# Seven block products instead of eight for gate and up of the first FFN, with weight sums on GpSimd and activations normalised ahead

## The chip, the cores and the metric

The kernel runs on one core of one Trainium2 chip. The profile names five engines: PE (TensorE, matmuls, with the weight loads as PEld), DVE (VectorE), ACT (ScalarE), POOL (GpSimd) and SP (SyncE, which here only issues DMAs). Matrix products land in PSUM banks, everything else lies in SBUF; weights and activations come from HBM by DMA. The metric is device time in microseconds of one execution, the median of several.

## The reference, cut to what matters

One layer of a hybrid decoder for 512 prompt tokens and 8 x 4 sample tokens, 544 in all, in float32:

```python
def swiglu(x, wg, wu, wd):
    return (jax.nn.silu(x @ wg) * (x @ wu)) @ wd

def layer(h, ...):
    h = h + 0.5 * rmsnorm(swiglu(rmsnorm(h, norm_g[0]), wg[0], wu[0], wd[0]), norm_g[1])
    m, c_kv, k_r, s_fin = mixer(rmsnorm(h, norm_g[2]), ...)
    h = h + rmsnorm(m, norm_g[3])
    h = h + 0.5 * rmsnorm(swiglu(rmsnorm(h, norm_g[4]), wg[1], wu[1], wd[1]), norm_g[5])
    return h, c_kv, k_r, s_fin
```

`wg` and `wu` are 1024 x 2816, `wd` is 2816 x 1024. The mixer (a gated linear recurrence beside latent attention over a paged cache) is the same in both kernels.

## The kernel before

Activations are kept transposed: 128 features on the partitions, tokens along the free axis, so `h[x]` is 128 x 8 x tokens. The 544 tokens are two halves, `x` = 0 of 256 and `x` = 1 of 288 (names ending in `a` and `b`). Float32 accuracy comes from splitting each operand in a high part, rounded to the matmul's type, and the remainder: `uh`/`ul` for activations, `wh`/`wl` for weights. A product of two split operands is three matmuls (high x high, high x low, low x high), written by `mm3`, `gemm` and `gemm_q` (L253, L271). One weight block of 1024 x 128 is loaded to `wraw` (five buffers, DMA on SP's queue), cast to `wh` on ACT (L244) and subtracted to `wl` on DVE (L245) by `weight`. So a block times one half of the tokens is 8 x 3 = 24 matmuls into one PSUM bank `acc`.

Start (scope `xin`): tokens are loaded as rows (`xt`), transposed by PE (L420) and copied to `h` (L423). Of the first norm only the gain is applied before the products (`split_u`, L202 and L203); the factor per token (`rstd_u`, L176 to L193) is worked out beside the first products and applied to their results (L343, and by the square in `post`).

The first FFN (`ffn`) runs in chunks of 8, 7 and 7 blocks of 128 hidden features. For each block: gate for both halves, up for both halves, then silu and product (`sil`, `sit`, L343 to L346, sigmoid as exp, ln, exp on ACT at L313 to L315) and a split into `hh`/`hl` (L165, L166). After a chunk, eight down groups, one per 128 output features, add into `mT` (`ma`, `mb`; L369 the first time, L371 later). In the last chunk the last five output features are taken half by half (staged weights `whx`, `wlx`), so that `post` can normalise the first half, add it to `h` (L305, L306) and make the mixer's `u` while PE works on the second half. Then the mixer starts with three weight blocks on half 0 and on half 1 (`zx`, L586).

The order of instructions on each engine is fixed at build time: a scheduler lays the program's operations out on in-order queues, and each waits there for its operands and for its buffers. SP's queue holds all weight loads in the order of use.

Of the kernel before, what the change touches and what calls it, by code (L numbers as in the profile page):

```python
# [8 lines left out]
F32 = mybir.dt.float32  # L9
# [17 lines left out]
HM = max(HS)  # L27
DFF = 2816
NF = DFF // P
FCH = (((0, 8), (8, 7), (15, 7)), ((0, 6), (6, 6), (12, 5), (17, 5)))  # L30
# [75 lines left out]
def hybrid_step_kernel(  # L106
# [14 lines left out]
    halves = (slice(0, HS[0]), slice(HS[0], T))  # L121
    BOTH = (0, 1)
# [22 lines left out]
    def actslot(name, x, dt=F32, shape=None):  # L145
        return mk(shape or [P, KD, HS[x]], dt, name + "ab"[x], pool=act)
# [3 lines left out]
    h = [actslot("h", x) for x in BOTH]  # L150

    def hslices(lo, n):
        out = []
        for x in BOTH:
            o = halves[x].start
            a, b = max(lo, o), min(lo + n, halves[x].stop)
            if a < b:
                out.append((x, slice(a - o, b - o), slice(a - lo, b - lo)))
        return out
# [45 lines left out]
    def parted_u(norm, x):  # L205
        u = actslot("uh", x, F32R), actslot("ul", x, F32R), tmp("rn" + "ab"[x], HS[x], 1)
# [91 lines left out]
    def post(x, mT, acc, r, nxt=None):  # L298
        s = tmp("s_post", HS[x])
# [3 lines left out]
        for k in range(0, KD, 2):  # L303
            ks = slice(k, k + 2)
            nc.vector.tensor_tensor(mT[:, ks], mT[:, ks], s[:, None, :].broadcast_to([P, 2, HS[x]]), op=ALU.mult)  # L305
# [3 lines left out]
            if k == 2:  # L309
                yield  # L310
# [93 lines left out]
    newb = mk([P, TS], BF16, "newb")  # L404
    with scope("xin"):
# [4 lines left out]
        nc.vector.tensor_copy(gv, pv[:, :V_N])  # L410

        def xload(tiles):
            for i in tiles:
# [3 lines left out]
                for q in range(2):  # L417
# [3 lines left out]
                    for x, dst, src in hslices(i * P, n):  # L421
                        eng = nc.scalar.copy if q else nc.vector.tensor_copy
                        eng(h[x][:, 4 * q : 4 * q + 4, dst], px.rearrange("p (k t) -> p k t", k=4)[:, :, src])  # L423

        w0, u0 = [], {}

        def first(c):
            w0.append(weight([wcols((w_g, w_u)[c][0], 0, KD, 0)], KD))

        xload((0, 1))  # L430
        if W0 == 0:
            first(0)
        u0[0] = split_u(0, 0)
        if W0 == 1:
            first(0)
        xload((2, 3, 4))
        first(1)
        u0[1] = split_u(0, 1)
        nc.vector.tensor_scalar_mul(gq, gv[:, 0:48], 0.5)
        for x in BOTH:  # L440
            rstd_u(u0[x], x)
# [26 lines left out]

    stg = ExitStack()
    st = stg.enter_context(tc.tile_pool(name="st", bufs=1, side="right", reuse_waits="tile"))  # L470
    with scope("ffn0"):
        U = [None, None]
        hsp = [dr.tile([P, KD, HS[x]], F32, name="hsp%d" % x, tag="hsp%d" % x) for x in BOTH]

        def to_mix(x):
            U[x], part = parted_u(2, x)
            return part

        first_w = []

        def mid():
            first_w.extend(weight([wcols(w_in, 0, KD, 2048 + i * P)], KD, True) for i in JOBS[:NST])

        for _ in ffn(0, 1, BOTH, u0, to_mix, mid):
            pass
        for x in BOTH:
            nc.sync.dma_start(hsp[x], h[x])
# [5 lines left out]
    def fetch(x, slot, src):  # L493
        h[x] = mk([P, KD, HS[x]], F32, slot, pool=act)
# [8 lines left out]
    def project(x, nxt=None):  # L503
        fetch(x, ("q0", "hb")[x], hsp[x])
# [30 lines left out]
    with scope("mix") as mx_:  # L535
# [5 lines left out]
        q0 = mk([P, 2, KQ, HS[0]], F32R, "q0", pool=act)  # L541
        q1 = mk([P, 2, KQ, HS[1]], F32R, "q1", pool=dK)
        qh, ql = (q0[:, 0], q1[:, 0]), (q0[:, 1], q1[:, 1])
        s_q = [mk([P, HS[x]], F32, "s_q%d" % x) for x in BOTH]

        def cq(j, a, x):
            scaled_split(qh[x][:, j], ql[x][:, j], a, gcol(V_QG + j))
            q = tmp("sq1", HS[x])
# [4 lines left out]
        def kvz(j, a, x):  # L553
            nc.scalar.copy(zkv[:, j, halves[x]], a)
# [27 lines left out]
        zx = [ps("zx")[:, : HS[1]] for _ in first]  # L582
# [19 lines left out]
        def hgrn(hd):  # L602
            def zcol(z, off):
                w = weight([wcols(w_in, 0, KD, off + hd * P)], KD)
                for x, hs in enumerate(halves):
# [216 lines left out]
        with scope("at2"):  # L822
# [7 lines left out]
            with scope("kv"):  # L830
# [5 lines left out]
                for x, hs in enumerate(halves):  # L836
# [603 lines left out]
```

## Time and profile before

| | |
|---|---|
| median of three runs | 1312.4 us (1311.62, 1312.40, 1316.96) |
| profiled execution: span, first to last instruction | 1312.7 us |
| its own time around the span | not listed apart; the span lies 0.3 us above the median |
| PE busy | 1288.4 us, 98% |
| DVE busy | 879.7 us, 67% |
| ACT busy | 713.9 us, 54% |
| POOL busy | 73.8 us, 6% |
| mean granted TensorE clock | 0.995 |
| HBM traffic over the span | 145 GB/s |

In a row of groups there stand the line, the engine, the operation, the output and the inputs, the shape (partitions x elements), the count, then busy time and mean duration of one, then the idle time in front and what ended it. Matmuls overlap one another, so the mean duration of a matmul is longer than the distance from one start to the next. A timeline row begins with the start and the duration in us. A row of a table by stage gives the stretch, its length, then busy time and number of instructions of PE, PEld, DVE, ACT and POOL, then the granted clock, the DMA engines' share and GB/s; a table cut to one line of code leaves out engines that have nothing there.

### The profile page before, as it was taken

How to read it: one execution, taken by the hardware profiler on the slowest of the kernel's cores; microseconds unless marked ns; L12 is line 12 of the kernel's file. 1: busy time of each engine (PE TensorE's matmuls, PEld its weight loads, DVE VectorE, ACT ScalarE, POOL GpSimd, SP SyncE). 2: the span in 40 equal slices, each digit the busy share in tenths (PEclk: the TensorE clock that was granted, in tenths of full speed). 3: DMA queues.
4: the chain of work that ended last, by engine and by line, in shares of the span. 5: the costliest groups of instructions: out<-in, count | busy, mean ns of one | idle time of the engine just before them, and what ended most of it. 6: DMA issues, size and time to landing. Idle time of an engine off the chain costs nothing.

```text
span 1312.7 us, 30501 instructions
## 1 busy us (share of the span) xinstructions
PE 1288.4 (98%) x12696; PEld 1196.2 (91%) x12696; DVE 879.7 (67%) x1765; ACT 713.9 (54%) x1503; POOL 73.8 (6%) x80
## 2 busy tenths in 40 slices
PE   7999999999999999999999999999999999999998
PEld 6999999999999988888987888878788999999997
DVE  7553244435457787875867789899987878466664
ACT  6543344324455644544758656665656677554454
POOL 0000000000000000000000222232310000000000
PEclk9999999999999999999999999999999999999998
DMA  7323233332353223333223687988886746656451
GB/s 217 90 81 96 82 88 85 85 98 81 88 154 113 95 65 84 84 85 114 59 86 96 239 285 244 300 276 278 283 268 183 222 137 178 177 144 186 137 158 55
DMA packets 280552, 192.87 MB, mean 147 GB/s; under 512 B 12765, under 2 KB 271422, under 8 KB 275550
## 3 DMA queue, kind: packets, MB, share of 16 engines
q1 hardware_dynamic: 271920, 147.65, 39.0%
q0 software_dynamic: 7168, 41.95, 8.7%
q8 instruction: 100, 1.64, 0.5%
q10 hardware_dynamic: 1326, 1.32, 0.3%
q14 instruction: 38, 0.31, 0.1%
HBM read 181.22 MB, written 9.67 MB: 145 GB/s over the span
## 4 chain that ended last, share of the span: by engine, by line
PE 85%; DVE 6%; ACT 5%; DMA 3%; issue 1%; SPq 0%; DVEq 0%; ACTq 0%
PE acc L253 54%; PE acc L271 16%; PE s L1141 3%; PE o L1174 2%; DVE wl L245 1%; ACT wh L244 1%; PE s L954 1%; PE pa L693 1%; DMA wraw<-w_d 1%; PE acc L282 1%; DMA wraw<-w_u 1%; PE zx L586 1%; ACT pbuf L1165 1%; PE pr L186 1%; PE o L986 1%
## 5 line engine op out<-in xcount | busy, mean ns | idle before, releaser
L244 ACT CAST wh<-wraw 128x1024 fp32r<-128x1024 f32 (+3 forms) x255 | 248.2, 976 | 296.4 <-PE acc L253 238.3
L245 DVE TENSOR_TENSOR wl<-wraw,wh 128x1024 fp32r<-128x1024 f32 (+3 forms) x255 | 288.7, 1133 | 147.9 <-ACT wh L244 147.4
L253 PE MATMUL acc<-uhb,wh 128*128 128x288 f32 x768 | 227.6, 296 | 0.6 <-ACT uhb L202 0.6
L253 PE MATMUL acc<-ulb,wh 128*128 128x288 f32 x768 | 227.1, 296 | 0.0
L253 PE MATMUL acc<-uhb,wl 128*128 128x288 f32 x768 | 225.7, 294 | 0.8 <-DVE wl L245 0.7
L271 PE MATMUL acc<-uha,wh 128*128 128x256 f32 x528 | 158.3, 301 | 1.0 <-ACT uha L202 1.0
L271 PE MATMUL acc<-uha,wl 128*128 128x256 f32 x528 | 149.7, 284 | 2.3 <-DVE wl L245 2.3
L271 PE MATMUL acc<-ula,wh 128*128 128x256 f32 x528 | 150.3, 285 | 0.0
L253 PEld LDWEIGHTS acc<-uhb,wl 128*128 128x128 f32 x768 | 144.4, 188 | 1.3 <-DVE wl L245 1.3
L253 PEld LDWEIGHTS acc<-uhb,wh 128*128 128x128 f32 x768 | 144.1, 188 | 1.4 <-ACT uhb L202 0.8
L253 PEld LDWEIGHTS acc<-ulb,wh 128*128 128x128 f32 x768 | 144.2, 188 | 0.1
L253 PE MATMUL acc<-uha,wh 128*128 128x256 f32 x416 | 117.8, 283 | 0.5 <-DVE sil L343 0.5
L253 PE MATMUL acc<-uha,wl 128*128 128x256 f32 x416 | 117.5, 283 | 0.7 <-DVE wl L245 0.7
L253 PE MATMUL acc<-ula,wh 128*128 128x256 f32 x416 | 117.2, 282 | 0.2 <-DVE ula L203 0.2
L271 PEld LDWEIGHTS acc<-uha,wh 128*128 128x128 f32 x528 | 99.8, 189 | 16.3 <-issue 14.0
L271 PEld LDWEIGHTS acc<-uha,wl 128*128 128x128 f32 x528 | 100.4, 190 | 3.7 <-DVE wl L245 3.2
L271 PEld LDWEIGHTS acc<-ula,wh 128*128 128x128 f32 x528 | 100.5, 191 | 1.1 <-issue 1.0
L253 PE MATMUL acc<-hhb,wh 128*128 128x288 f32 x317 | 93.5, 297 | 0.6 <-ACT hhb L165 0.6
L253 PE MATMUL acc<-hlb,wh 128*128 128x288 f32 x317 | 93.9, 297 | 0.1
L253 PE MATMUL acc<-hhb,wl 128*128 128x288 f32 x317 | 92.9, 294 | 0.0
L253 PEld LDWEIGHTS acc<-uha,wl 128*128 128x128 f32 x416 | 78.3, 188 | 1.1 <-DVE wl L245 1.1
L253 PEld LDWEIGHTS acc<-uha,wh 128*128 128x128 f32 x416 | 78.4, 188 | 0.8 <-DVE sil L343 0.8
(483 smaller groups left out, 2926.4 us busy)
## 6 DMA issues: line engine op xcount, KB each, us to landing
wraw<-w_g SPq DMA_DIRECT2D x66, 512.0 KB, 4.5
wraw<-w_u SPq DMA_DIRECT2D x66, 512.0 KB, 4.0
wraw<-w_in SPq DMA_DIRECT2D x24, 512.0 KB, 4.0
wraw<-w_d SPq DMA_DIRECT2D x32, 384.0 KB, 4.4
wraw<-w_d SPq DMA_DIRECT2D x32, 320.0 KB, 3.3
wraw<-w_o SPq DMA_DIRECT2D x16, 512.0 KB, 4.1
wraw<-w_d SPq DMA_DIRECT2D x16, 448.0 KB, 3.8
wraw<-w_d SPq DMA_DIRECT2D x8, 512.0 KB, 4.0
```

What stands on the lines that cost most here:

```text
L186: nc.tensor.matmul(pr[:, :n], ones, acc, start=True, stop=True)
L244: nc.scalar.copy(wh[:, :kt], w[:, :kt])
L245: nc.vector.tensor_tensor(wl[:, :kt], w[:, :kt], f32(wh[:, :kt]), op=ALU.subtract)
L253: nc.tensor.matmul(out, a, b, start=n == 0, stop=n == last)
L271: nc.tensor.matmul(acc[:, :n], a[:, k], b[:, k], start=k + i == 0, stop=k == kt - 1 and i == 2)
L282: nc.tensor.matmul(acc, a[:, k], b[:, k], start=k + i == 0, stop=k == kt - 1 and i == 2)
L586: nc.tensor.matmul(z, w[a][:, k], U[1][b][:, k], start=k + n == 0, stop=k == KD - 1 and n == 2)
L693: nc.tensor.matmul(pa[es, c * 32 : (c + 1) * 32].rearrange("p (n m) -> p n m", m=m), kx[:, cs], up(qx[:, cs]), start=True, stop=True, skip ...
L954: nc.tensor.matmul(s[:, :N], qa[a_], ka[b_], start=n == 0, stop=False, skip_group_check=True)
L986: nc.tensor.matmul(o[:, lo : 2 * P], a_[:, k, hs], b_[:, k, lo:], start=n == 0, stop=n == 3 * q0 + 5, skip_group_check=True)
L1141: nc.tensor.matmul(self.s[r][c * 32 : c * 32 + 32, :P], q[rs, j], kh, start=st + jj == 0, stop=st == len(JS) - 1 and jj == 1, skip_group_c ...
L1174: nc.tensor.matmul(o[g : g + 32, :R], self.p[:, c, a], self.craw[c][:, a], start=i + c == 0 and a < 4, stop=i + c == 2 and a >= 4, skip_gr ...
```

## The change

Gate and up of the first FFN are worked out in pairs of blocks. For a pair, the weights are a 2 x 2 matrix of blocks (lower and upper four of the eight k tiles by first and second column block, `w1` and `w2`), and the activations another (lower and upper k tiles by first and second half of the tokens). Seven products of sums replace the eight block products (Winograd's form of Strassen's scheme). The halves become even, 272 and 272, all through the first FFN and the mixer's first stages; `project` and the second FFN keep 256 and 288.

- `xin`: each token row is squared and summed on ACT (L452), its factor made by Ln and Exp, spread over the partitions by a matmul with the identity (L456) and copied to `rb` (L457); `ux` = `h` times gain times factor (L462, L467), then split. `h` is written out to HBM (`hx`) and its slots (`ha`, `hb`) hold the gate and up results, until it is loaded again for `post`.
- `classic`: the first pair of gate and of up still takes 96 matmuls. Beside it the four activation sums are built (L598, two on POOL, two on DVE) and split to T1 to T4.
- `seven`: four sums of weight blocks on POOL (L541 to L544), seven splits of 128 x 512 (cast on ACT L168, subtraction on DVE L169), seven products of 12 matmuls (L536) into the banks X, Y and Z, two copies out of X (L562, L566) and five additions (L559). `issue_after` ties the later splits behind the previous pair's first copy.
- `gated`: sigmoid, two products and the split, for both halves at once (128 x 544; L318 to L320, L584, L585).
- Chunks of 6, 6, 6 and 4 blocks instead of 8, 7 and 7.

On DVE inside gate/up, there stood for each block two splits of 1024, and for each half three steps of the gating and a split:

```order
L343 TENSOR_TENSOR sil<-acc,rna 128x256
L345 TENSOR_TENSOR sil<-sil,sit 128x256
L343 TENSOR_TENSOR sil<-acc,rnb 128x288
L245 TENSOR_TENSOR wl<-wraw,wh 128x1024
L345 TENSOR_TENSOR sil<-sil,sit 128x288
L346 TENSOR_TENSOR sil<-sil,acc 128x256
L166 TENSOR_TENSOR hla<-sil,hha 128x256
L346 TENSOR_TENSOR sil<-sil,acc 128x288
```

Now, for the gate of one pair at a chunk's start (`ha` is the gate's result, `Y` and `Z` banks, `tq` the copy of X, `S` the sums from POOL, `s4` the last of them):

```order
L559 TENSOR_TENSOR ha<-Y,tq 128x272
L169 TENSOR_TENSOR wl<-S,wh 128x512 x2
L559 TENSOR_TENSOR ha<-Y,tq 128x272
L559 TENSOR_TENSOR ha<-Z,ha 128x272
L169 TENSOR_TENSOR sl<-wraw,sh 128x512 x2
L559 TENSOR_TENSOR ha<-Y,tq 128x272
L169 TENSOR_TENSOR sl<-wraw,sh 128x512 x2
L559 TENSOR_TENSOR ha<-Z,ha 128x272
```

The additions that empty the banks now stand between splits, some of which take POOL's results.

On ACT at the start, before (up to the first half's `u`):

```order
L448 ACTIVATE lbe<-lbe 128x8
L423 COPY ha<-px 128x4x128
L244 CAST wh<-wraw 128x1024
L423 COPY ha<-px 128x4x128
L202 ACTIVATE uha<-ha,gv 128x256 x8
```

and now, from the second token tile on (`xq` is a scratch output, `rows` the sums and factors):

```order
L452 ACTIVATE xq,rows<-xt 128x1024
L449 COPY ha<-px 128x4x128
L454 ACTIVATE rows<-rows 128x1
L453 ACTIVATE rows<-rows,epst 128x1
L479 ACTIVATE lbe<-lbe 128x8
L168 CAST wh<-wraw 128x1024
L449 COPY ha<-px 128x4x16
L449 COPY hb<-px 128x4x112
L454 ACTIVATE rows<-rows 128x1
L168 CAST sh<-wraw 128x1024
L452 ACTIVATE xq,rows<-xt 128x1024
L168 CAST uha<-ma 128x272 x5
```

The casts of the first half now stand behind the Squares and behind two weight casts.

On POOL, whose queue held nothing between the mask cast and the mixer, each `seven` now has four operations in a row (`S` the sums, `wraw` overwritten in place):

```order
L541 TENSOR_TENSOR S<-wraw 128x512
L542 TENSOR_TENSOR S<-S,wraw 128x512
L543 TENSOR_TENSOR wraw<-wraw 128x512
L544 TENSOR_TENSOR S<-wraw,S 128x512
```

Each waits for the one ahead or for both weight blocks; the splits above wait for them.

The core of the diff:

```diff
+W2 = T // 2
+WARM = 1
-FCH = (((0, 8), (8, 7), (15, 7)), ((0, 6), (6, 6), (12, 5), (17, 5)))
+FCH = (((0, 6), (6, 6), (12, 6), (18, 4)), ((0, 6), (6, 6), (12, 5), (17, 5)))
...
+                sq = mk([P, D], F32, "xq", 2)
+                r = rows[:n, i : i + 1]
+                nc.scalar.activation(sq[:n], xt[:n], AF.Square, accum_out=r)
+                nc.scalar.activation(r, r, AF.Ln, scale=1.0 / D, bias=epst[:n])
+                nc.scalar.activation(r, r, AF.Exp, scale=-0.5)
+                pr = ps("pr")
+                nc.tensor.matmul(pr[:, :n], r.broadcast_to([n, P]), ident[:n, :n], start=True, stop=True)
+                nc.vector.tensor_copy(rb[:, i * P : i * P + n], pr[:, :n])
...
+        for k in range(KD):
+            nc.vector.scalar_tensor_tensor(ux[0][:, k], h[0][:, k], gcol(k), rb[:, even[0]], op0=ALU.mult, op1=ALU.mult)
+            split(UB[0][0][:, k], UB[0][1][:, k], ux[0][:, k])
...
-        for _ in ffn(0, 1, BOTH, u0, to_mix, mid):
-            pass
...
+        def product(bank, a, b, first):
+            for k in range(4):
+                for n, (p, q) in enumerate(((0, 0), (0, 1), (1, 0))):
+                    nc.tensor.matmul(bank, a[p][:, k], b[q][:, k], start=first and k + n == 0, stop=k == 3 and n == 2, skip_group_check=True)
...
+        def seven(w, C, mid=None):
+            w1, w2 = w
+            S = mk([P, 3, 4, P], F32, "S", 2)
+            nc.gpsimd.tensor_tensor(S[:, 0], w2[:, lo4], w2[:, hi4], op=ALU.add)
+            nc.gpsimd.tensor_tensor(S[:, 1], S[:, 0], w1[:, lo4], op=ALU.subtract)
+            nc.gpsimd.tensor_tensor(w2[:, lo4], w1[:, lo4], w2[:, lo4], op=ALU.subtract)
+            nc.gpsimd.tensor_tensor(S[:, 2], w1[:, hi4], S[:, 1], op=ALU.subtract)
+            a, s, v = ring(), ring(), ring()
+            for ks in (lo4, hi4):
+                split(*parts(a, ks), w1[:, ks])
+            for i, ks in enumerate((lo4, hi4)):
+                split(*parts(s, ks), S[:, i])
+            s4 = [mk([P, 4, P], F32R, "s4" + n, 2, pool=sp) for n in "hl"]
+            with tc.issue_after(mark[0]):
+                for ks in (lo4, hi4):
+                    split(*parts(v, ks), w2[:, ks])
+                split(*s4, S[:, 2])
...
+            product(X, parts(a, lo4), B11, True)
+            mark[0] = nc.scalar.copy(t, X).ins
+            product(Y, parts(s, hi4), T2, True)
+            plus(1, Y, t)
+            product(X, parts(a, hi4), B21, False)
+            nc.scalar.copy(C[:, 0], X)
...
+            product(Y, parts(v, lo4), T3, False)
+            plus(3, Y, t)
+            product(Z, parts(s, lo4), T1, True)
+            plus(3, Z, C[:, 3])
+            product(Y, parts(v, hi4), T4, False)
+            plus(2, Y, t)
+            product(Z, s4, B22, False)
+            plus(1, Z, C[:, 1])
...
+                    seven(raw_pair(w_g[0], f0 + j), G, (lambda: split(*T4, r[0])) if f0 + j == 2 * WARM else None)
+                    if late:
+                        with tc.issue_after(mark[0]):
+                            gated(*late)
+                    seven(raw_pair(w_u[0], f0 + j), V)
+                late = j, G, V
+            gated(*late)
```

200 lines of the change are left out of this document (147 added, 53 removed).

## The prediction

> **What bounds the kernel now.** I read the page's busy times and chain first, then a table by stage, then the timeline inside one stage.
>
> ```profile
> span 1312.7 us, 30501 instructions
> PE 1288.4 (98%) x12696; PEld 1196.2 (91%) x12696; DVE 879.7 (67%) x1765; ACT 713.9 (54%) x1503; POOL 73.8 (6%) x80
> PE 85%; DVE 6%; ACT 5%; DMA 3%; issue 1%; SPq 0%; DVEq 0%; ACTq 0%
> ```
>
> TensorE (PE) is busy nearly all the span and holds 85% of the chain; POOL (GpSimd) does next to nothing. Next, the first FFN: two tables of stretches, the first counting only the matmuls of L253 (gate, up, down and the mixer's first products), the second all work in two gate/up stretches and one down stretch.
>
> ```profile
> 0.00:31.82 31.82, 17.43 (x121) 15.57 (x121) 1.00 0.77 217
> 31.82:355.62 323.80, 323.80 (x2569) 323.80 (x2570) 1.00 0.31 88
> 355.62:428.31 72.69, 70.42 (x553) 69.13 (x552) 1.00 0.44 127
> ```
> ```profile
> 40.00:110.00 70.00, 70.00 (x558) 70.00 (x557) 34.02 (x57) 32.51 (x59) 0.00 (x0) 1.00 0.31 89
> 122.00:154.00 32.00, 32.00 (x256) 32.00 (x255) 6.24 (x6) 8.97 (x16) 0.00 (x0) 1.00 0.29 84
> ```
>
> The three stretches hold 121 + 2569 + 553 = 3243 matmuls. The FFN's own are 22 x 2 x 48 = 2112 for gate and up and 22 x 8 x 6 = 1056 for down; 72 more are the mixer's first. In the middle stretch they start every 323.80 / 2569 = 0.126 us with no gap, at full granted clock. VectorE (DVE) and ScalarE (ACT) are about half busy in gate/up. So this stage is bound by the number of matmuls, and a matmul removed is 0.126 us less as long as the others keep up. The mean durations in the groups (280 to 300 ns) are not that price, because matmuls overlap; starts are:
>
> ```profile
> 100.00 0.29 PE L253 MATMUL acc<-uhb,wh 128*128 128x288 f32 x1
> 101.60 0.28 PE L253 MATMUL acc<-uha,wh 128*128 128x256 f32 x1
> 102.78 0.28 PE L253 MATMUL acc<-ula,wh 128*128 128x256 f32 x1
> ```
>
> Twelve matmuls of 288 columns lie between the first two rows (0.133 us each), ten of 256 between the others (0.118 us each). Both are 0.46 ns a column, so two halves of 272 cost what 256 + 288 cost, 0.126 us on average, and the even halves neither gain nor lose anywhere in the kernel.
>
> **The change, part by part.** Prices that the sums use:
>
> ```profile
> L245 DVE TENSOR_TENSOR wl<-wraw,wh 128x1024 fp32r<-128x1024 f32 x59 | 72.3, 1226 | 62.5 <-ACT wh L244 62.5
> L305 DVE TENSOR_TENSOR ma<-ma,s_post 128x512 f32<-128x512 f32 x4 | 2.7, 687 | 0.0
> L622 DVE TENSOR_TENSOR g_q<-g_q,g_sg 128x544 f32<-128x544 f32 x2 | 1.4, 722 | 2.0 <-ACT g_sg L315 2.0
> L371 DVE TENSOR_TENSOR mb<-mb,acc 128x288 f32<-128x288 f32 x16 | 7.2, 453 | 22.1 <-PE acc L253 22.1
> L244 ACT CAST wh<-wraw 128x1024 fp32r<-128x1024 f32 x59 | 61.7, 1046 | 94.3 <-PE acc L253 92.0 <-PE acc L271 1.1 <-DMA wraw<-w_in 0.9
> L678 ACT ACTIVATE g_E<-g_E 128x512 f32<-128x512 f32 x4 | 2.5, 625 | 0.7 <-DVE g_E L677 0.7
> L314 ACT ACTIVATE g_sg<-g_sg,ones 128x544 f32<-128x544 f32 x3 | 2.2, 736 | 0.0
> L1341 POOL TENSOR_TENSOR q<-q,mt 128x512 f32<-128x512 f32 x1 | 1.3, 1260 | 331.1 <-ACT mt L1340 331.1
> ```
>
> 1. Matmuls removed. A pair of blocks of 128 columns took 96 matmuls and takes 7 x 12 = 84. The first pair of gate and of up stays at 96, so 20 pairs save 12 each: 240 x 0.126 = 30.2 us. This is on the path. The Trainium skill ("TensorE: Matmul & The Clock Gate", Back-to-back issue gap) gives an isolated gap of 272 / 2.4 + 2.5 = 116 ns for 272 columns, which would make the saving 27.8 us; the starts above say 126 ns, and the trace decides.
>
> 2. What has to keep up. Per gate-and-up couple of pairs PE now takes 168 x 0.126 = 21.2 us, where it took 192 x 0.126 = 24.2. In it DVE does 14 subtractions of 128x512 for the weight parts (14 x 0.69 = 9.6), ten additions out of PSUM at 272 columns (L371, 0.44 between its two sizes: 4.4) and six operations of 128x544 for the gating (6 x 0.72 = 4.3): 18.3 us. ACT does 14 casts (0.58, between half of L244 and L678: 8.1), four copies (about 0.4, 1.6), six steps of the sigmoid (L314 at most, 4.4) and two casts of 544 (1.3): 15.4 us. POOL does eight sums and differences at 1.26: 10.1 us. Each alone is below 21.2, though DVE goes from 34.02 / 70 = 49% to 86%. The down stretches leave DVE four fifths idle (6.24 of 32 us), and by the order nine of a chunk's first splits and eight POOL operations are issued in them.
>
> 3. New waits of PE. Four banks per seven products are emptied and taken again: X must be copied before product 3, Y emptied before products 4 and 6, Z before product 7. In each case one product (12 x 0.126 = 1.51 us) runs between, and the emptying takes 0.44, so DVE may come 1.07 us late; a split in front of it is 0.69. Alone this fits, and I take 0; with some POOL operations in the way I take 0.05 us on each of the 80 places, 4 us in all. Nearest rows for the ends: nothing is late (0), or one split behind one POOL operation at every second place: (0.69 + 1.26 - 1.07) x 40 = 35 us. I take the value near the first end, because DVE has 2.9 us to spare per couple.
>
> 4. Start. Normalising ahead puts three Squares of 1024, their Ln and Exp, and three copies on ACT, ahead of the first normalised tile. Rows of before:
>
> ```profile
> 5.03 0.29 PEld L420 LDWEIGHTS px<-ident,xt 128*128 128x128 f32 x2 [5.03 <-DMA xt<-x_p]
> 7.16 0.21 ACT L448 ACTIVATE lbe<-lbe 128x8 f32<-128x8 f32 x1 [5.15 <-DVE lbe L447]
> 7.28 0.57 ACT L423 COPY ha<-px 128x512 f32<-128x512 f32 x1
> 10.19 3.25 DVE L203 SCALAR_TENSOR_TENSOR ula<-ha,gv,uha 128x256 fp32r<-128x256 f32 x8
> 27.98 0.38 PE L253 MATMUL acc<-uha,wh 128*128 128x256 f32 x1 [0.53 <-DVE sil L343]
> ```
>
> From 5.0 on, ACT has three Squares (3 x 1.05), three copies (1.7), one weight cast (1.05) and seven small ones (0.21 each): 12.4 us, and the factor reaches DVE near 13.2. DVE then has two weight splits (2.5), 16 scalings at 3.25 / 8 = 0.41 (6.5), 16 subtractions (about 0.38: 6.0) and copies (1.8): the 96 matmuls of the first gate pair cannot end before 30.0, where before 96 were done at 28.0. Before, though, PE then still waited for its norms (17.43 us busy up to 31.82, 121 matmuls); by 31.82 the new kernel would have done 96 + 14 = 110. That is 11 x 0.126 = 1.4 us, with about 1 us for the first split of seven products: +2.5. Ends: -1 (the waits of before cost more than I count) and +8 (the x tiles land late behind two weight tiles on SP's queue). The two spills of h are issued on SP ahead of the third pair's weights; these are needed only some 12 us later (96 x 0.126).
>
> 5. Chunks. Four down stretches instead of three split the same 1056 matmuls, with 16 more additions (L371), hidden under PE. Behind the last product of a chunk, addition, gating multiply, cast and subtraction need 0.44 + 0.72 + 0.65 + 0.72 = 2.5 us before the last block's part is there; the order puts 24 matmuls of two down groups in front (3.0 us). Price 0, at most 4 x 2 us.
>
> 6. The seam into the mixer. Before:
>
> ```profile
> 406.12 14.45 PE acc L253 x111
> 421.25 6.54 PE acc L253 x55
> 428.31 9.15 PE zx L586 x69
> ```
> ```profile
> 404.00:437.50 33.50, 33.45 (x256) 32.88 (x255) 28.86 (x57) 21.02 (x46) 0.00 (x0) 1.00 0.39 131
> ```
>
> PE covers the norm of the first half with five groups of the second (14.45 us) and is never idle, while DVE is 28.86 of 33.50 us busy. In the last chunk of four blocks these five groups are 5 x 12 x 0.126 = 7.6 us. By the order DVE has some 17 us of work between the end of the first half's sums and its last part of u: four splits (4.6), eight 544s (5.4), eight scalings (3.3) and eleven 272s (4.1). The mixer's first 72 matmuls (9.1 us) follow these parts, and the next 72 those of the other half, at about 27.5. PE's work from there is 7.6 + 18.1 = 25.7, DVE's last part plus two matmul groups about 29.5: +4 us, ends 0 and +8. The reload of h (2.2 MB) stands on SP behind all of w_d and needs only the gating's end.
>
> Behind the seam the same number of columns runs, and queues read almost alike: 0, +-3.
>
> Sum against this execution's span: 1312.7 - 30.2 + 4 + 2.5 + 4 = 1293.0 us. The span is 0.3 above the median of the three runs (1312.4), so I leave it: **1293 us**, 1.5% faster.
>
> **The rivals.** B, DVE and POOL exclude each other. If a DVE operation with two SBUF operands and a POOL operation never run together, a couple needs 13.9 + 10.1 = 24.0 us, with DVE's PSUM work serial too 28.4, against 21.2 for PE. Over ten couples that is 240 to 284; what the three inner down stretches take ahead (nine splits and eight POOL operations each, 3 x 16.3 = 49) leaves 191 to 235 against 212. So 0 to 23 us come back, 12 in the middle: 1305. No row of before shows it: its one POOL addition (L1341) runs with DVE idle. The Trainium skill ("SBUF — State Buffer", Who interferes with whom) states just this rule: the later of the two waits for the other's whole instruction. No run so far bears it out or refutes it.
>
> C, slower: the same exclusion strikes in the four bank waits of item 3. A split that waits out a POOL operation and then holds up the addition costs 0.88 us there. It decides when the mean over the 80 places passes (30.2 - 6.5) / 80 = 0.30 us, one place in three; at half of them 1312.7 - 23.7 + 35 = 1324. For it speaks DVE's 86% and an order fixed before the run, against it POOL's 48% and the down stretches in which DVE catches up.
>
> D, the gain is spent at the seams (items 4, 5, 6 at their upper ends, 8 + 8 + 8, with 4 of item 3): 1310. For it speaks that DVE is nearly full at both; against it that each end needs its own delay.
>
> The change not doing what it says is out on PE's side: its queue holds 240 matmuls fewer.
>
> **How the numbers follow.** Forecast 0.50, B 0.20, C 0.18, D 0.12. Faster by over 0.5% (below 1306, about what a measurement can tell) are nearly all of the forecast, half of B and a quarter of D: 0.63. Within 0.5%: 0.02 of the forecast, the rest of B and most of D: 0.17. Slower: C and a little of B and D: 0.20. The forecast's own range is 1285 to 1303; to leave out 2 in 10 the range reaches down to 1284 and up to 1322, into C.
>
> **What would show it.** PE's matmuls in the first FFN: 240 fewer; 0.126 us apart inside a product; the mixer's zx group begins near 409 instead of 428. Wrong if idle of PE before products 3, 4, 6 or 7 adds up to more than 10 us, if DVE's 128x512 subtraction takes well over 0.69 us (B, C), if the steady stream begins after 36 us, or if PE stands still over 8 us between the last down group and zx.

## The result and the profile after

The changed kernel took 1314.8 us (median of 12 runs), the kernel before 1315.3 us on the same chip (median of 12): a ratio of 0.9994, 95% interval 0.998 to 1.0008. One of the changed kernel's twelve executions took 4038 us and is left out of the ratio. There is no change that can be measured; 1293 us, 1.5% faster, had been forecast. The page of the changed kernel answers to the lines shown of before:

```profile
span 1312.5 us, 30382 instructions
PE 1270.6 (97%) x12462; PEld 1174.6 (89%) x12462; DVE 989.0 (75%) x1891; ACT 745.6 (57%) x1576; POOL 205.0 (16%) x162
PE 76%; DVE 12%; ACT 5%; issue 3%; DMA 2%; POOL 1%; SPq 0%; DVEq 0%; POOLq 0%; ACTq 0%
```

PE has 234 recorded matmuls fewer, and its busy time falls by 18 us, but the span stays: PE's share of the chain falls from 85% to 76%, and DVE's doubles to 12%. A table by stage of the changed kernel shows where (the columns are busy time and count of PE, PEld, DVE, ACT and POOL, then the granted clock):

```profile
14.80:47.30 32.50, 30.36 (x205) 29.42 (x205) 28.11 (x46) 17.33 (x39) 16.18 (x9) 0.86 0.65 186
47.30:66.70 19.40, 13.02 (x87) 12.27 (x86) 17.57 (x19) 10.80 (x21) 13.05 (x7) 0.82 0.09 27
...
271.70:287.10 15.40, 12.36 (x87) 12.14 (x86) 14.06 (x19) 4.90 (x10) 6.61 (x4) 0.89 0.26 77
287.10:297.60 10.50, 10.50 (x87) 10.50 (x86) 6.31 (x12) 8.67 (x16) 0.00 (x0) 1.00 0.15 39
386.90:430.60 43.70, 39.55 (x280) 37.14 (x279) 36.23 (x69) 30.57 (x63) 0.00 (x0) 0.96 0.76 213
```

The fourth row is a set of seven products as forecast: 10.5 us for 84 matmuls, 0.125 us each, without a gap. The second row is the very first set (19.4 us), the third is the set for the second couple's up products in the third chunk (15.4 us). In both, POOL works beside a DVE that is nearly always busy. In the fourth row POOL is idle.

To compare kernels, the first FFN is cut in three, and in each part what its matmuls need at 0.1255 us each is subtracted. "Start" is the time at which 192 matmuls (the first gate and up pairs) are done, less 24.1 us; "sets" is the time from there to the last chunk's down groups, less its matmuls; "seam" the time from there to the first zx matmul, less its matmuls. Starts of matmuls in the timeline give:

| lost time in us | start | sets | seam | zx begins |
|---|---|---|---|---|
| before | 17.0 | 1.3 | 2.7 | 427.6 |
| changed | 23.2 | 20.4 | 9.3 | 430.6 |
| difference | +6.2 | +19.1 | +6.6 | +3.0 |

The 1.3 us of before are no wait: its matmuls of 256 and 288 columns start 0.126 us apart on average, a little more than those of 272. 30.1 us of matmuls are saved, 31.9 us newly lost, and ten matmuls (1.3 us) are done ahead of zx, so zx begins 3.0 us later. Behind that the changed kernel is 3.2 us shorter (1.3 of it are those ten matmuls; the rest was not looked into), and so the spans agree. The forecast had +2.5, +4 and +4. It failed most at the sets: 19.1 us instead of 4.

One bank wait shows how. DVE, POOL and PE of the changed kernel around 275 us (timeline rows: start, duration, engine):

```profile
274.59 0.69 DVE L169 TENSOR_TENSOR sl<-wraw,sh 128x512 fp32r<-128x512 f32 x1
275.19 0.43 DVE L559 TENSOR_TENSOR hb<-Y,tq 128x272 f32<-128x272 f32 x1
275.54 1.43 DVE L169 TENSOR_TENSOR sl<-wraw,sh 128x512 fp32r<-128x512 f32 x1
276.89 1.79 DVE L169 TENSOR_TENSOR s4l<-S,s4h 128x512 fp32r<-128x512 f32 x1
278.60 3.44 DVE L169 TENSOR_TENSOR wl<-S,wh 128x512 fp32r<-128x512 f32 x2
281.96 0.43 DVE L559 TENSOR_TENSOR hb<-Y,tq 128x272 f32<-128x272 f32 x1
```
```profile
274.81 1.61 POOL L541 TENSOR_TENSOR S<-wraw 128x512 f32<-128x512 f32 x1 [10.62 <-DVE s4l L169]
276.50 1.63 POOL L542 TENSOR_TENSOR S<-S,wraw 128x512 f32<-128x512 f32 x1
278.09 1.73 POOL L543 TENSOR_TENSOR wraw<-wraw 128x512 f32<-128x512 f32 x1
279.78 1.71 POOL L544 TENSOR_TENSOR S<-wraw,S 128x512 f32<-128x512 f32 x1
```
```profile
279.12 0.29 PE L536 MATMUL Z<-uhb,wl 128*128 128x272 f32 x1
282.44 0.40 PE L536 MATMUL Y<-t4h,sh 128*128 128x272 f32 x1 [3.04 <-DVE hb L559]
```

A DVE subtraction that nothing holds up takes 0.69 us, and the next operation starts 0.60 us later (first row). From 275.5 on, where POOL makes its sums, DVE's subtractions start 1.4 to 1.7 us apart and POOL's sums 1.6 to 1.7 (274.81, 276.50, 278.09, 279.78; one alone takes 1.26, below): the two engines take turns. The four splits between the additions of `hb` take 6.4 us instead of 2.4, the addition that empties bank Y comes late, and product 6 waits 3.04 us for it. The addition itself reads PSUM and takes 0.43 us with POOL beside it or without.

The groups by shape show the same over the whole kernel (count, busy us, mean ns):

```profile
L169 DVE TENSOR_TENSOR wl<-wraw,wh 128x512 fp32r<-128x512 f32 x40 | 41.6, 1069 | 6.1 <-ACT wh L168 5.3
L169 DVE TENSOR_TENSOR sl<-wraw,sh 128x512 fp32r<-128x512 f32 x40 | 40.0, 1033 | 3.5 <-ACT sh L168 2.9
...
L543 POOL TENSOR_TENSOR wraw<-wraw 128x512 f32<-128x512 f32 x20 | 34.2, 1711 | 0.0
...
L1496 POOL TENSOR_TENSOR q<-q,mt 128x512 f32<-128x512 f32 x1 | 1.3, 1259 | 331.4 <-ACT mt L1495 331.4
```

Taken one by one, 78 of the 140 subtractions of 128x512 that make weight parts have no sum of POOL's beside them and take 0.68 us on average, 0.70 at most. The 62 others take 1.35 us on average, up to 1.80.

### The profile page after: what moved, and what is told of

Its sections match the earlier page's. It is cut to its first block, busy times and chain, and to the rows that moved or that the text cites. A ratio compares the mean times of both kernels' runs of the same rounds, so it can differ in the third digit from the quotient of the medians.

```text
span 1312.5 us, 30382 instructions
## 1 busy us (share of the span) xinstructions
PE 1270.6 (97%) x12462; PEld 1174.6 (89%) x12462; DVE 989.0 (75%) x1891; ACT 745.6 (57%) x1576; POOL 205.0 (16%) x162
## 4 chain that ended last, share of the span: by engine, by line
PE 76%; DVE 12%; ACT 5%; issue 3%; DMA 2%; POOL 1%; SPq 0%; DVEq 0%; POOLq 0%; ACTq 0%
PE acc L257 35%; PE acc L275 16%; PE Y L536 5%; PE Z L536 3%; PE X L536 3%; PE s L1296 3%; PE o L1329 2%; DVE sl L169 2%; DVE wl L249 1%; DVE wl L169 1%; ACT wh L248 1%; PE s L1109 1%; PE pa L846 1%; PE acc L286 1%; DVE kh L1284 1%
## 5 line engine op out<-in xcount | busy, mean ns | idle before, releaser
L275 PE MATMUL acc<-uha,wh 128*128 128x256 f32 (+1 forms) x528 | 159.6, 303 | 1.2 <-ACT uha L205 0.9
L275 PE MATMUL acc<-uha,wl 128*128 128x256 f32 (+1 forms) x528 | 151.1, 287 | 1.9 <-DVE wl L249 1.9
L275 PE MATMUL acc<-ula,wh 128*128 128x256 f32 (+1 forms) x528 | 151.5, 287 | 0.0
L257 PE MATMUL acc<-uhb,wh 128*128 128x288 f32 (+1 forms) x424 | 126.1, 297 | 0.1
L257 PE MATMUL acc<-ulb,wh 128*128 128x288 f32 (+1 forms) x424 | 125.3, 296 | 0.0
L257 PE MATMUL acc<-uhb,wl 128*128 128x288 f32 (+1 forms) x424 | 124.6, 295 | 0.5 <-DVE wl L249 0.3
L275 PEld LDWEIGHTS acc<-uha,wh 128*128 128x128 f32 x528 | 100.5, 191 | 15.9 <-issue 13.5
L275 PEld LDWEIGHTS acc<-uha,wl 128*128 128x128 f32 x528 | 100.4, 190 | 3.0 <-DVE wl L249 2.7
L257 PEld LDWEIGHTS acc<-uhb,wl 128*128 128x128 f32 x424 | 79.7, 188 | 1.2 <-DVE wl L249 1.2
L257 PEld LDWEIGHTS acc<-uhb,wh 128*128 128x128 f32 x424 | 79.5, 187 | 0.7 <-ACT wh L248 0.3
L541 POOL TENSOR_TENSOR S<-wraw 128x512 f32<-128x512 f32 x20 | 27.7, 1384 | 198.8 <-DMA wraw<-w_g 52.4
```

The lines of the kernel that those rows point to most:

```text
L257: nc.tensor.matmul(out, a, b, start=n == 0, stop=n == last)
L275: nc.tensor.matmul(acc[:, :n], a[:, k], b[:, k], start=k + i == 0, stop=k == kt - 1 and i == 2)
L541: nc.gpsimd.tensor_tensor(S[:, 0], w2[:, lo4], w2[:, hi4], op=ALU.add)
```

## The experiments

The theory from the traces was: of the gain, 6.5 us go at the start, 9.7 in the first set (with the half clock behind it), 8 in two bank waits and 8.5 at the seam; the losses in the sets come from the sums on POOL. Against it stood exclusion alone (rival B), and the start and the seam alone. The kernels ran on more than one chip, and the kernel before took 1315 to 1328 us, depending on the chip; each is set against the kernel before on its own chip. The table collects all; the parts follow.

| kernel | start | sets | seam | zx begins | against before (95%) |
|---|---|---|---|---|---|
| changed, again | 23.5 | 19.1 | 10.5 | 430.9 | 0.9998 (0.9983 to 1.0013) |
| no sums | 21.2 | 0.4 | 11.1 | 410.5 | 0.9847 (0.9827 to 0.9867) |
| sums made, not read | 23.4 | 15.7 | 10.5 | 427.4 | 0.9956 (0.9940 to 0.9972) |
| memsets, not read | 23.3 | 2.2 | 10.0 | 413.3 | 0.9837 (0.9806 to 0.9869) |
| sums on DVE | 23.9 | 2.0 | 10.7 | 414.4 | 0.9858 (0.9834 to 0.9882) |
| T1, T2 on DVE | 20.5 | 20.0 | 10.8 | 429.1 | 0.9992 (0.9970 to 1.0014) |
| second couple as eight | 22.4 | 10.0 | 8.8 | 423.7 | 0.9956 (0.9940 to 0.9972) |
| all as eight | 20.6 | 0.5 | 9.5 | 438.4 | 1.0042 (1.0026 to 1.0059) |
| a quarter of h | 22.4 | 20.2 | 8.6 | 428.9 | 0.9980 (0.9966 to 0.9994) |
| last chunk of six | 21.8 | 24.7 | 5.0 | 429.2 | 0.9983 (0.9964 to 1.0001) |
| sums on DVE, last of six | 23.6 | 2.9 | 5.0 | 409.2 | 0.9818 (0.9772 to 0.9864) |
| sums on DVE, PE kept busy | 22.9 | 1.1 | 9.6 | 411.4 | 0.9845 (0.9805 to 0.9884) |

The changed kernel, run again beside others, gave what was expected; it also shows how far single traces differ (0.3 to 1.3 us in a part).

> The changed kernel itself, on the same chip as the three others, so that they can be set against it there: no change to before (within 0.3%), with the same four losses.

### What the sums on POOL cost

No sums:

```diff
-            nc.gpsimd.tensor_tensor(S[:, 0], w2[:, lo4], w2[:, hi4], op=ALU.add)
-            nc.gpsimd.tensor_tensor(S[:, 1], S[:, 0], w1[:, lo4], op=ALU.subtract)
-            nc.gpsimd.tensor_tensor(w2[:, lo4], w1[:, lo4], w2[:, lo4], op=ALU.subtract)
-            nc.gpsimd.tensor_tensor(S[:, 2], w1[:, hi4], S[:, 1], op=ALU.subtract)
...
-                split(*parts(s, ks), S[:, i])
+                split(*parts(s, ks), w2[:, ks])
...
-                split(*s4, S[:, 2])
+                split(*s4, w1[:, hi4])
```

> The four POOL sums and differences of each seven-product pair are left out: the parts are split from the raw weight blocks themselves, so that DVE, ACT and PE issue the same instructions as in the changed kernel and only POOL's 160 are gone; what is computed is therefore not the reference's product. Theory (the gain is given back at four places, 6.5 us at the start, 9.7 in the first seven products, 8 at two bank waits in chunks 1 and 2, 8.5 at the seam): the bank waits and about half of the first seven's loss go, the start and the seam stay, so about 1302 us (12 faster than the changed kernel), and a DVE subtraction of 128x512 falls from 1.03 to about 0.69 us. Rival B as forecast (exclusion alone takes the gain): 1285 us, all 30 back. Rival without POOL in it (start and seam alone): within 3 us of the changed kernel.

Measured: 1.5% faster than before (20 us), 8 more than the theory's 12. (The instructions left out are 80, four in each of 20 sets, not 160.) Every set took 10.5 to 11.0 us, the first one too, and the subtractions fell to 0.69 us:

```profile
45.30:55.90 10.60, 10.60 (x87) 10.60 (x86) 8.18 (x14) 10.50 (x20) 0.00 (x0) 1.00 0.36 99
```
```profile
L169 DVE TENSOR_TENSOR wl<-wraw,wh 128x512 fp32r<-128x512 f32 x60 | 39.8, 687 | 15.9 <-ACT wh L168 14.3
```

So the sums cost all of the 20 us lost in the sets. That zx then begins at 410.5, where the prediction had 409, is in part luck: the start and the seam lose 12.6 us more than in before (21.2 against 17.0 and 11.1 against 2.7) where 6.5 were forecast, and the forecast 4 us in the sets are missing. Still open was whether the parts wait for the sums, or DVE for POOL.

Sums made, not read, and memsets in their place (both on top of the kernel without sums):

```diff
+            S = mk([P, 3, 4, P], F32, "S", 2)
+            nc.gpsimd.tensor_tensor(S[:, 0], w2[:, lo4], w2[:, hi4], op=ALU.add)
+            nc.gpsimd.tensor_tensor(S[:, 1], S[:, 0], w1[:, lo4], op=ALU.subtract)
+            nc.gpsimd.tensor_tensor(S[:, 0], w1[:, lo4], w2[:, lo4], op=ALU.subtract)
+            nc.gpsimd.tensor_tensor(S[:, 2], w1[:, hi4], S[:, 1], op=ALU.subtract)
```
```diff
+            S = mk([P, 3, 4, P], F32, "S", 2)
+            nc.gpsimd.tensor_copy(S[:, 0, 0, :1], w2[:, 0, :1])
+            for i in (0, 1, 2, 0, 1, 2, 0, 1):
+                nc.gpsimd.memset(S[:, i], 0.0)
```

> As the kernel without sums (parts split from the raw weight blocks, so not the reference's product), but POOL computes the four sums and differences of each pair all the same, into S, which nobody reads: POOL's load is that of the changed kernel, and DVE's and ACT's order is that of the kernel without sums, in which nothing waits for a sum. The kernel without sums was 1.5% faster than the kernel before. Theory A (what the sums cost is the exclusion: DVE and POOL stretch each other): most of it comes back, at least 10 of the 20 us, 0.2 to 0.8% faster than before, and the 128x512 subtractions take about 1.0 us in the mean. Theory B (what they cost is that the parts wait for the sums, a chain of up to three POOL operations): it stays at 1.5% faster, within 0.25%, with the subtractions long or not.

> As the kernel without sums (parts split from the raw weight blocks, so not the reference's product), but POOL sets S, which nobody reads, to zero eight times per pair (128x512 each) behind one element copied from the pair's second block, so that it is busy at the same places as with the unread sums, and only writes SBUF. Theory A, narrow (DVE and POOL exclude each other where both read SBUF): the 128x512 subtractions stay near 0.69 us in the mean, the first seven products near 10.5 us, and the kernel near 1.5% faster than before, as without sums. Theory A, wide (any POOL work on SBUF holds DVE up): the subtractions take 0.85 us or more, the first seven products 14 us or more, and the kernel is at most 1.0% faster than before.

Measured: with unread sums 15.7 of the 20.4 us in the sets are lost again, although DVE and ACT issue the same instructions in the same order as without sums and wait for no result of POOL's but T1's and T2's. With memsets 2.2 us are lost, most of it in the first set (12.5 us, where 10.5 was expected: T2's sum stands behind memsets in POOL's queue). The first set of each, and the groups, of the unread sums:

```profile
47.50:66.70 19.20, 13.04 (x87) 12.29 (x86) 16.84 (x18) 10.04 (x20) 11.96 (x7) 0.82 0.20 55
```
```profile
L169 DVE TENSOR_TENSOR sl<-wraw,sh 128x512 fp32r<-128x512 f32 x60 | 60.3, 1028 | 8.2 <-ACT sh L168 6.9
```

and of the memsets:

```profile
L169 DVE TENSOR_TENSOR sl<-wraw,sh 128x512 fp32r<-128x512 f32 x60 | 39.7, 685 | 10.6 <-ACT sh L168 9.2
```
```profile
L543 POOL MEMSET S<- 128x512 f32 x160 | 76.1, 526 | 4.6 <-ACT wh L168 4.5
```
```profile
46.70 5.67 POOL L543 MEMSET S<- 128x512 f32 x12
```
```profile
50.22 0.68 DVE L169 TENSOR_TENSOR sl<-wraw,sh 128x512 fp32r<-128x512 f32 x1
50.82 0.68 DVE L169 TENSOR_TENSOR wl<-wraw,wh 128x512 fp32r<-128x512 f32 x1
```

So it is the exclusion, in its narrow form: in these traces a DVE operation with two SBUF inputs and a POOL operation that reads SBUF take turns (0.69 against 1.03 us), and a POOL operation that only writes does not slow DVE. That POOL holds the weight buffers longer is not the reason: from 47 to 400 us ACT's casts of the sets' blocks (L168) wait 5.2 us for loads with unread sums and 5.6 us without sums. One reservation: 160 memsets kept POOL busy for 76 us, about six tenths of the sums' 126, and some ran ahead of the places where the sums would stand. Beside the twelve from 46.70 to 52.37, though, DVE's subtractions kept 0.68 us. The Trainium skill ("SBUF — State Buffer", Who interferes with whom) states exactly this rule, with the same exception for writes; here the traces bear it out. The 15.7 us do not all stand where the changed kernel loses its 20.4, however. The first set is the same (19.2 us), but the two long bank waits of 2.9 and 3.0 us are gone, in place of eight of 0.5 to 1.1. So unread sums show the cause for the first set; for the two long waits it rests on the rows around 275 us, where DVE has no gap between the two additions and four splits take 6.4 us instead of 2.4. What waiting for the sums' results adds was not separated.

Sums on DVE:

```diff
-            nc.gpsimd.tensor_tensor(S[:, 0], w2[:, lo4], w2[:, hi4], op=ALU.add)
+            nc.vector.tensor_tensor(S[:, 0], w2[:, lo4], w2[:, hi4], op=ALU.add)
...
```

> The four sums and differences of each pair are made on DVE in place of POOL; all else as in the changed kernel. By rows, a couple then needs 18.3 + 8 x 0.69 = 23.8 us of DVE against 21.2 of PE, with the down stretches to catch up in. Theory A (exclusion: a sum on POOL costs DVE its whole 1.1 us, on DVE only 0.69, and the chain of three gets shorter): 3 to 10 us faster than the changed kernel. Theory B (POOL works beside DVE and only latency counts, DVE's own load becomes the bound): (23.8 - 21.2) x 10 couples, less what the down stretches take, so up to 26 us slower than the changed kernel, 10 in the middle.

Measured: 1.4% faster than before and 19 us faster than the changed kernel, where the theory had 3 to 10, with the whole result computed. DVE has 80 operations more, and yet it is only as busy as in the changed kernel (989.3 us against 989.0):

```profile
PE 1271.4 (97%) x12462; PEld 1171.6 (90%) x12462; DVE 989.3 (76%) x1971; ACT 745.4 (57%) x1576; POOL 79.6 (6%) x82
```
```profile
259.40:270.00 10.60, 10.60 (x87) 10.60 (x86) 10.52 (x21) 4.93 (x10) 0.00 (x0) 1.00 0.26 77
```

That is what the exclusion costs in DVE's time: 80 sums on POOL lengthened DVE's work as much as 80 sums on DVE do, 989.0 - 942.6 (the kernel without sums) = 46 us. The second row is the up set that stands where the changed kernel's bank wait was: DVE is busy 10.52 of 10.60 us, all sums included, and PE does not wait. Theory B, by which DVE would become the bound at 23.8 us a couple against 21.2, fell too: the down stretches take the difference, as the sets lose only 2.0 us.

So DVE's load as such is not what costs. With the same 989 us the sets lose 2.0 us here and 20.4 in the changed kernel. A sum on DVE takes 0.60 us at its own place in the queue; a sum on POOL puts up to 1.10 us on each split that it meets, four in a row, also right in front of an addition that PE waits for. But the order on DVE's queue and the time at which a sum is there differ between the two kernels as well, and no run separates these three.

### The first set

The first set loses 8.9 us in the changed kernel. DVE's parts of the activation sums (T3, T2) take 2.36 and 2.38 us there, and T2's sum is made on POOL behind the four weight sums. T1 and T2 on DVE instead:

```diff
-                    for e, o, p, q, dst in ((nc.gpsimd, l[0], l[1], l[0], T1), (nc.vector, l[1], r[1], l[1], T3), (nc.gpsimd, r[1], r[1], l[0], T2), (nc.vector, r[0], r[0], r[1], T4)):
+                    for e, o, p, q, dst in ((nc.vector, l[0], l[1], l[0], T1), (nc.vector, l[1], r[1], l[1], T3), (nc.vector, r[1], r[1], l[0], T2), (nc.vector, r[0], r[0], r[1], T4)):
```

> The changed kernel with its two activation differences that POOL makes (T1 and T2, 128x1088 each) made on DVE instead; the weight sums stay on POOL. Theory (the 19.4 us of the first seven products, where 10.5 are undisturbed, come from T2's place in POOL's queue behind the chain of four sums): the first seven products take 12 us or less, and the kernel is 6 to 8 us faster than the changed one, 0.4 to 0.6% below before. Rival (they come from DVE being stretched by POOL, whoever makes T2): the first seven products still take over 16 us, and the time is within 3 us of the changed kernel.

Measured: the first set still takes 19.3 us, and the time is that of before. The theory (T2's place in POOL's queue) fell, the rival holds. DVE in that stretch, in this kernel and, in the second fence, in the one with the sums on DVE:

```profile
41.16 2.38 DVE L169 TENSOR_TENSOR t3l<-mb,t3h 128x1088 fp32r<-128x1088 f32 x1
43.47 2.38 DVE L598 TENSOR_TENSOR ma<-ma,mb 128x1088 f32<-128x1088 f32 x1
45.77 2.37 DVE L169 TENSOR_TENSOR t2l<-mb,t2h 128x1088 fp32r<-128x1088 f32 x1
```
```profile
42.07 1.28 DVE L169 TENSOR_TENSOR t3l<-mb,t3h 128x1088 fp32r<-128x1088 f32 x1
43.27 1.28 DVE L169 TENSOR_TENSOR t2l<-mb,t2h 128x1088 fp32r<-128x1088 f32 x1
```

Each takes 1.10 us more when POOL is at its weight sums, nearly the length of one sum (1.26 us). DVE has the first set's splits and the activation parts to do just then, with no slack.

The second couple as eight products gives it that slack:

```diff
-WARM = 1
+WARM = 2
...
+                    if f0 + j < 2 * WARM - 2:
+                        late = j, G, V
+                        continue
```

> The second couple of pairs too is done as eight products, so that the four activation differences and their parts have a couple's time (24 us) to be built before the first seven products need them: 24 more matmuls, 3.0 us. Theory: most of the 9.7 us lost in the first seven products goes, 1314.8 + 3.0 - 8 = 1310 us. Rival (the loss is that of any first seven products behind a classic couple, since their sums start late): it moves to the second couple, 1318 us.

Measured as expected: 0.4% faster than before, the first set 10.5 us, 24 matmuls more. The bank waits of the second and third chunks stay (two of 3 us). This removes the loss at one place, not its cause.

### The start and the seam

All as eight products:

```diff
-WARM = 1
+WARM = 11
...
```

> All 22 pairs are done as eight products, in the changed kernel's chunks, start and seam; no sums are built. Theory: PE has the 240 matmuls again (+30.2 us) and loses neither the 9.7 us of the first seven products nor the 8 us at the bank waits, so 1314.8 + 30.2 - 17.7 = 1327 us, that is, the start and the seam alone make it 12 to 15 us slower than the kernel before. Rival (the seven products lose the gain everywhere by exclusion, and the rest costs nothing): 1315 us, as before.

Measured: 0.4% slower than before, 5.6 us (3.5 to 7.8), where the theory had 12 to 15. By the stage the theory was near: zx begins 10.8 us later than in before. But 5 us of it come back behind zx, as 3.2 did in the changed kernel; what gives them back was not looked into.

A quarter of h at the seam:

```diff
-                    nc.sync.dma_start(h[x], hx[:, :, even[x]])
+                    nc.sync.dma_start(h[x][:, :2], hx[:, :2, even[x]])
+                    nc.gpsimd.memset(h[x][:, 2:], 0.0)
```

> At the seam a quarter of h is loaded again (two of eight blocks of each half) and the rest is set to zero by POOL, so that 1.6 MB less stand ahead of the mixer's weights in SP's queue; the residual is therefore not the reference's from there on. Theory (the mixer's weights land late behind h, and ACT's cast of them holds the Squares of the first half): the weights land some 5 us sooner, and 3 to 5 us of the 8.5 us at the seam come back, 1310 to 1312 us. Rival (the seam goes at DVE's pace whatever lands when): within 1 us of the changed kernel.

Measured: 0.2% faster than before, and the seam loses 8.6 us, where kernels with the same seam lose 8.8 to 11.1. The 3 to 5 us of the theory are not seen; that the mixer's weights land late behind h explains 1 to 2 us at most, and by the seam alone perhaps nothing.

Last chunk of six blocks, with the sums on POOL and with the sums on DVE:

```diff
-FCH = (((0, 6), (6, 6), (12, 6), (18, 4)), ((0, 6), (6, 6), (12, 5), (17, 5)))
+FCH = (((0, 6), (6, 6), (12, 4), (16, 6)), ((0, 6), (6, 6), (12, 5), (17, 5)))
```

> The chunks are 6, 6, 4 and 6 blocks instead of 6, 6, 6 and 4, so that the last group of five down products covers the norm of the first half with 5 x 18 x 0.126 = 11.3 us instead of 7.6. Theory (the seam goes at the pace of DVE behind too short a cover, as cutting the reload of h to a quarter left most of its loss): 3 to 4 us faster than the changed kernel, PE's idle time between the last down group and the zx group from 8 us to about 4. Rival (the order of the queues makes it, whatever the cover): unchanged.

> The sums on DVE, which alone is 1.4% faster than before, and chunks of 6, 6, 4 and 6 blocks. With the sums on POOL this order of chunks took 4.3 us off the seam's loss (9.3 to 5.0) and gave 2.7 back in bank waits. Theory (bank waits are POOL's doing): with the sums on DVE the seam's gain stays, 3 to 5 us faster than the kernel with sums on DVE, 1.7% below before. Rival (the shorter third down stretch leaves DVE, now with 23.8 us of work per couple of 21.2, no time to catch up): bank waits come back in the last chunk, within 1 us of the kernel with sums on DVE or slower.

Measured: the seam's loss falls from 9.3 to 5.0 us in both, as expected: what is short there is PE's cover for DVE's work on the norm. With the sums on POOL the last chunk gets new bank waits (the sets lose 24.7 us instead of 20.4), and little is left of the gain (0.9983, against 0.9998 for the changed kernel on the same chip). With the sums on DVE it stays. The page, and the row of the seam (PE alone):

```profile
span 1290.1 us, 30320 instructions
PE 1258.5 (98%) x12462; PEld 1167.2 (90%) x12462; DVE 987.8 (77%) x1971; ACT 745.8 (58%) x1576; POOL 81.3 (6%) x82
PE 81%; DVE 10%; ACT 4%; DMA 2%; issue 2%; POOL 0%; DVEq 0%; SPq 0%; ACTq 0%; POOLq 0%
```
```profile
357.80:409.20 51.40, 48.13 (x376) 1.00 0.67 193
```

This version, with the whole result computed, beats both kernels: 1292.5 us against 1315.5 of before on the same chip, 0.9818 (0.9772 to 0.9864). By the times alone its step from the kernel with sums on DVE (0.9858) is not clear of noise; the traces show it, with zx 5.2 us sooner. Part of the seam's gain is the clock: 1.00 in this row, 0.96 in the changed kernel's, which has 3.4 us at half clock there.

PE kept busy at the start (on top of the sums on DVE; 16 unread matmuls on the identity behind the first token tiles, 8 between the first pair's halves):

```diff
+        def fill(n):
+            pd = ps("pd")
+            for _ in range(n):
+                nc.tensor.matmul(pd[:, :P], ident, ident, start=True, stop=True)
...
         xload((0, 1, 2))
+        fill(16)
...
```

> The sums on DVE, and 24 matmuls of 128x128 on constants whose result nobody reads, put into PE's queue where PE stood idle at the start (16 at 10.5 to 13.5 us, 8 between the first pair's two halves). Theory (the half clock of 14 to 21 and 24 to 28 us in the changed kernel follows these idle stretches, and costs 2 to 4 us of the 6.5 us that the start loses): the granted clock stays at 1.00 up to 30 us, and the first seven products begin 2 to 4 us sooner than with the sums on DVE alone (48.0). Rival (DVE and ACT are full at the start and set it, so a faster PE only waits): the clock stays up, and the first seven products begin within 1 us of 48.0.

Stretches of 5 us from 10 to 25, first of the changed kernel, then of this one (PE alone, clock behind it):

```profile
10.00:15.00 5.00, 3.20 (x18) 0.89 1.12 309
15.00:20.00 5.00, 5.00 (x23) 0.50 0.99 289
20.00:25.00 5.00, 3.58 (x24) 0.84 0.30 105
```
```profile
10.00:15.00 5.00, 5.00 (x45) 1.00 1.12 299
15.00:20.00 5.00, 5.00 (x42) 1.00 0.97 282
20.00:25.00 5.00, 5.00 (x42) 1.00 0.77 226
```

Measured: the clock stays full up to 30 us (from 31.8 to 35.2 it is halved), and the first set begins at 47.0 instead of 48.0. That is within the spread of single traces: in the changed kernel, its second run and two others with the same start it begins at 45.9 to 47.6. The 2 to 4 us of the theory are not there, and the rival holds: a faster PE waits. The half clock there is a result of the waiting more than a cause of the loss.

One cause at the start stands in rows that no run was made for. T1's sum on POOL falls beside DVE's scalings of the second half, which read two operands from SBUF. First the changed kernel, then the one with T1 and T2 on DVE:

```profile
25.83 3.60 DVE L467 SCALAR_TENSOR_TENSOR mb<-hb,gv,rb 128x272 f32<-128x272 f32 x3
26.48 2.65 POOL L598 TENSOR_TENSOR ma<-mb,ma 128x1088 f32<-128x1088 f32 x1 [26.04 <-DVE mb L467]
```
```profile
24.28 1.32 DVE L467 SCALAR_TENSOR_TENSOR mb<-hb,gv,rb 128x272 f32<-128x272 f32 x3
```

Three scalings take 2.3 us longer: the exclusion again. The two kernels without T1 on POOL lose 20.5 and 20.6 us at the start, all others with the changed start 21.2 to 23.9. T1 and T2 on DVE together with the weight sums on DVE were not run.

## Why the prediction was wrong

- Item 1, matmuls removed: right. 0.1255 us each, 240 fewer.
- Item 2, what has to keep up: this is the step that failed. "Each alone is below 21.2" adds up each engine by itself, as if POOL's sums cost DVE nothing. POOL's 10.1 us and DVE's two-input work do not run beside each other: the 46 us by which POOL's sums lengthen DVE's work are 4.6 a couple, and 18.3 + 4.6 = 22.9 is above PE's 21.2. This mean is not yet the loss, since with the sums on DVE a couple is as full and the sets lose 2.0 us. The loss stands where the longer splits come in bursts in front of what PE waits for.
- Item 3, bank waits: the term that was mis-sized by it, +4 forecast and +19.1 measured in the sets (20.4 against 1.3), inside its ends of 0 and 35. The price of 0.05 us on 80 places was the wrong picture: most places cost nothing, the first set costs 8.9 (DVE late for T3, T2 and the splits), the second 1.6, two bank waits 3.1 and 4.9 with the half clock behind the longer one, and four more 0.5 each. That "a split in front of it is 0.69" was too little as well: at the two long waits four splits stand there in the fixed order, 2.4 us alone and 6.4 beside POOL.
- Item 4, the start: +2.5 forecast, +6.2 measured, inside its ends (-1 to +8). By 31.8 us the changed kernel has done 70 matmuls, where the item had 110; before has 192 done by 41.1, the changed kernel by 47.3. Up to 2.3 us of it are T1's sum on POOL, at most about 1 us is the clock, and the rest was not taken apart.
- Item 5, chunks: right, about 0.2 us each.
- Item 6, the seam: +4 forecast, +6.6 measured, inside its ends (0 to +8). The mechanism was right: a cover of 7.6 us is too short, and 11.3 us takes 4.3 off.
- "Later 0, +-3": -3.2, just past its edge; without the ten matmuls done ahead it is -1.9.
- The rivals: B was the mechanism, with 0.20, and its 0 to 23 us took in the 19.1; its middle of 12 did not. Its way of pricing, DVE's load over ten couples, was not what decided. C named the right place (a split behind a POOL operation, then the addition), but not the concentration in three places. D's seams brought 12.8 of its 24 us. It took B near its top and half of D together to use up the gain; each alone would have left the kernel faster.
- The last paragraph's signs: subtractions of 1.03 to 1.07 us stood in the trace. PE was idle 8.4 us in front of products 3 to 7, short of the 10 named, and 5.4 us more inside the second product of the first set, a place that the prediction did not list. The seam lost 9.3 us, but PE stood still for only 4.2 of them; in the rest its matmuls start further apart.

## What to carry to other kernels

Before work is moved to POOL as "free", add its time to DVE's wherever POOL reads SBUF and DVE has two SBUF inputs; if DVE can do the same operation in half the time, as here (0.60 against 1.26 us), giving it to POOL frees nothing. This holds for the operations shown here, and a POOL operation that only writes is another case. An average slack per stage (2.9 us a couple) does not cover a burst: look for the place where the order puts several stretched operations in front of the one that PE waits for. And a saving on PE shortens the cover of everything that hides behind PE, so the last chunk wants its size chosen for that cover.

## What was not expected of the hardware

- Where the two meet, exclusion costs DVE nearly the POOL operation's own length (1.26 us), operation by operation: +1.10 us on a 128x1088 subtraction (1.28 to 2.38) and on a 128x512 one (0.60 to 1.70 from start to start), while additions with one PSUM operand keep 0.43 us.
- The clock can fall after short waits. Behind the 3.04 us wait above, matmuls of 272 columns start 0.23 us apart instead of 0.126 for 3.4 us:

```profile
284.46 0.43 PE L536 MATMUL Z<-uhb,s4h 128*128 128x272 f32 x1
284.69 0.43 PE L536 MATMUL Z<-ulb,s4h 128*128 128x272 f32 x1
```

Behind the other long bank wait (2.87 us) the clock stays full. In the changed kernel, run again, it is the other way round: it falls behind 2.87 us and not behind 2.90. So the length of a wait alone does not decide.

The Trainium skill ("TensorE: Matmul & The Clock Gate", Part 1: The HAM clock gate) names an idle window of about 3.4 us and a half clock. The half clock agrees (0.50 in the row 15.00:20.00 above); that a wait of 3.04 us, and at the start 3 us in which PE was partly busy, sufficed is shorter than the figure.
- A one-element copy on POOL, in the kernel with memsets, took 5.54 us while DVE ran two-input operations back to back. POOL's spans are rough, so this is only a hint that POOL can wait out more than one DVE operation.
